# An mLSTM and MLA encoder layer: tokens transposed before their RMS norm, the norm applied to the projections' results, and the opening loads issued at once

## The chip, the cores and the metric

One core of one Trainium2 chip. The metric is the device time of one execution in microseconds, median of three runs. The core has a matrix engine (PE, with its weight loader PEld), a vector engine (DVE), a scalar engine (ACT), a pool engine (POOL) and a sync engine (SP) that here issues nearly all transfers; every engine works through its own instructions in order and waits for others by semaphores.

## The reference

```python
h = rms_norm(x, g_mix)                   # x: 2048 x 1024, float32
z = h @ w_in                             # one projection, split into ten streams
q_m, k_m, v_m, o_m, gates, c_q, c_kv, k_pe = split(z)
qk  = silu(conv_centred([q_m, k_m]))     # depthwise conv of width 5 along the tokens
y_a = mlstm_group(qk, v_m, o_m, gates)   # bidirectional chunkwise mLSTM, 4 heads
y_b = mla_group(c_q, c_kv, k_pe, ...)    # latent attention, 4 heads, full softmax
x = x + concat(y_a, y_b) @ w_out
x = x + square(relu(rms_norm(x, g_ffn) @ w_ff1)) @ w_ff2
def rms_norm(x, g):
    return x * rsqrt(mean(x * x, -1) + 1e-6) * g
```

The norm's factor is one number per token. So `(x * r) @ w` and `(x @ w) * r` are the same but for rounding: the factor can be put on the rows of x or on the rows of the product.

## The kernel before

The program runs in phases; the change lies in `phase_a` alone, which ends at about 464 us of the span. It makes `z = h @ w_in` and its streams. The instructions of `phase_a` are put in order, engine by engine, by a scheduler that simulates the program; the later phases are ordered by hand, and their code is not touched. So the place of an instruction in a queue of `phase_a` is not the place of its line in the code.

Every float32 matrix product is made as three fp32r products (`mm3`, L67 to L69): each operand is split into a high part (`hh`, `wh`), cast by ACT (L52, L55), and a low part (`hl`, `wl`), the rest, which DVE subtracts (L53, L56). A product is hi by hi, hi by lo, lo by hi.

The 2048 tokens are 16 tiles of 128, in two halves of eight. `load_x` loads a tile `xt`; `prep` takes its mean square on ACT (`xjunk`, L145), the inverse root on POOL (`rsqrt`, L62 and L63), multiplies the tile by it on DVE (L148), and transposes it on PE in two groups of four blocks (`pt`, L153), each group being split into `hh` and `hl`, in which 512 tokens lie side by side. For each half, PE then goes through four blocks of columns of `w_in`, each block being eight row tiles k0 to k7 that `load_w` loads (`raw`, L161, three buffers) and splits:

- `rest`: the 464 columns of the gates and of the latents, called CR in the code, one `pz` of 24 matmuls per token tile. DVE adds a bias to the gates (`G`, L259), ACT copies the others (`zr`, L264).
- `z_v` (CV): 512 columns; DVE copies the result (L450) and SP stores it.
- `z_qk` (CQ): here the channels are on the partitions and 512 tokens are the columns. ACT copies the result into `zc` (L407), DVE does the five taps of the conv (L413 to L415).
- `z_o` (CO): ACT takes the sigmoid straight from PSUM (`vo`, L456), DVE multiplies by a gain.

Between them stand the steps of MLA's latents (`mla_a1` to `mla_b2`), by `tick`, and the splits of MLA's up-projections w_uq and w_ukv (`load_wu`: `wuqh`, `wuql`, `wukh`, `wukl`), whose raw tiles use the same three `raw` buffers.

At the very start, SP issues x0, the rows of `g_mix` (turned into columns on PE at L182, since `split` of the weights multiplies by g), three weight tiles, x1, small vectors, and then the further weight tiles as buffers come free.

A form that the change uses is in the kernel already, in the attention: a small SBUF tile with tokens on its partitions is stored to DRAM transposed (`d_rd`, L1036, 128x2, with `rearrange("a p -> p a")`), and read back spread over all partitions (`rb`, L1041).

Of the kernel before, what the change touches and what calls it, by code (L numbers as in the profile page):

```python
# [8 lines left out]
F32 = mybir.dt.float32  # L9
F32R = mybir.dt.float32r  # L10
# [76 lines left out]
def scratch(c, ctx):  # L87
    tc = c.tc
    dr = ctx.enter_context(tc.tile_pool(name="scratch", bufs=1, space=DRAM))
    c.d_qkT = dr.tile([4, P, S], F32, name="d_qkT")  # L90
    c.d_k = dr.tile([S, 256], F32, name="d_k")
    c.d_v = dr.tile([S, 512], F32, name="d_v")
    c.d_sg = dr.tile([S, 512], F32, name="d_sg")
    c.d_qn = dr.tile([NH, P, S], F32, name="d_qn")
    c.d_kn = dr.tile([NH, P, S], F32, name="d_kn")
    c.d_qr = dr.tile([NH, ROPE, S], F32, name="d_qr")
    c.d_kr = dr.tile([NH, ROPE, S], F32, name="d_kr")
    c.d_va = dr.tile([S, 512], F32, name="d_va")
# [17 lines left out]
def phase_a(c):  # L116
    nc, tc = c.nc, c.tc
    with ExitStack() as st:
# [16 lines left out]
        psM = pool("a_psM", 4, space=PSUM)  # L135

        def load_x(t):
            xt = xp.tile([P, D], F32, name="xt")
            nc.sync.dma_start(xt, c.x[t * P:(t + 1) * P, :])
            return xt  # L140

        def prep(t, xt, hh, hl):
            junk = ep.tile([P, D], BF16, name="xjunk", bufs=1)
            ms = sp.tile([P, 1], F32, name="xms")
            nc.scalar.activation(junk, xt, AF.Square, scale=D ** -0.5, accum_out=ms)  # L145
            r = sp.tile([P, 1], F32, name="xr")
            rsqrt(c, r, ms, 1)
            nc.vector.tensor_scalar(xt, xt, r, None, op0=ALU.mult)  # L148
            tt = t % 4
            for g in range(2):  # L150
                pt = psT.tile([P, 4, P], F32, name="pt")
                for k in range(4):
                    nc.tensor.transpose(pt[:, k, :], xt[:, (4 * g + k) * P:(4 * g + k + 1) * P], c.ident)  # L153
                split(nc, hh[:, 4 * g:4 * g + 4, tt * P:(tt + 1) * P],
                      hl[:, 4 * g:4 * g + 4, tt * P:(tt + 1) * P], pt)

        def load_w(c0, n):
            res = []
            for k in range(KD):
                raw = rp.tile([P, 512], F32, name="raw")  # L160
                nc.sync.dma_start(raw[:, :n], c.w_in[k * P:(k + 1) * P, c0:c0 + n])  # L161
                wh = wp.tile([P, 512], F32R, name="wh")
                wl = wp.tile([P, 512], F32R, name="wl")
                split(nc, wh[:, :n], wl[:, :n], raw[:, :n], gmix[:, k:k + 1])
                res.append((wh, wl))
            return res

        def vec_rows(name, srcs, q):

            rows = kp.tile([64, P], F32, name=name)  # L170
            nr = 0
            for src in srcs:
                if len(src.shape) == 2:
                    src = src.rearrange("a b -> (a b)")
                n = src.shape[0] // P
                q.dma_start(rows[nr:nr + n, :], src.rearrange("(r p) -> r p", p=P))
                nr += n
            return rows, nr

        def vec_cols(c0, rows, nr):  # L180
            pt = psT.tile([P, 4, P], F32, name="pt")
            nc.tensor.transpose(pt[:, 0, :nr], rows[:nr, :], c.ident[:nr, :nr])  # L182
            nc.vector.tensor_copy(c.vec[:, c0:c0 + nr], pt[:, 0, :nr])

        xts = {0: load_x(0)}
        gmix, gcq, cb = c.vec[:, 0:8], c.vec[:, 8:11], c.vec[:, 11:15]
        cw = c.vec[:, 15:35].rearrange("p (k c) -> p c k", c=4)
        c.gffn = c.vec[:, 35:43]
        vec_cols(0, *vec_rows("rows0", (c.g_mix,), nc.sync))
        posi = kp.tile([NT, P], I32, name="posi")  # L190
        gq = kp.tile([P, DH], F32, name="gq")
        gk = kp.tile([P, DH], F32, name="gk")
# [63 lines left out]
        def rest(t, hts, w):  # L256
            pz = z_nat(hts, t % 8, w, NR)
            for half, ci in ((0, t), (2, NT - 1 - t)):
                nc.vector.tensor_tensor(  # L259
                    c.G[:, half:half + 2, :, ci],  # L260
                    pz[:, half * 4:half * 4 + 8].rearrange("p (a h) -> p a h", a=2),
                    bg[:, half * 4:half * 4 + 8].rearrange("p (a h) -> p a h", a=2), op=ALU.add)
            zr = zp.tile([P, 448], F32, name="zr")
            nc.scalar.copy(zr, pz[:, 16:NR])  # L264
            return zr

        def rope(dst, src, t, nh, tmp):
# [12 lines left out]

        def mla_a1(t, zr):

            junk = mp.tile([P, 256], BF16, name="mjunk1")
# [18 lines left out]
        def mla_a2(t):  # L302
# [16 lines left out]
            junk = mp.tile([P, 256], BF16, name="mjunk2")  # L319
# [73 lines left out]
        def z_qk(j, ch, hts, w):  # L393
# [10 lines left out]
                nc.vector.memset(zc[:, 0:4], 0.0)  # L404
            else:
                nc.vector.tensor_copy(zc[:, 0:4], carry[:, ch, :])
            nc.scalar.copy(zc[:, 4:516], pz)  # L407
            if last:
                nc.vector.memset(zc[:, 516:518], 0.0)
            else:  # L410
# [16 lines left out]
            if ch >= 2:  # L427
# [12 lines left out]
                if last:  # L440
                    pt = psT.tile([P, 4, P], F32, name="pt")
                    nc.tensor.transpose(pt[0:2, 0, :], ot[:, 512:514], c.ident)
                    k2 = ep.tile([2, P], F32, name="k2", bufs=1)
                    nc.scalar.copy(k2, pt[0:2, 0, :])
                    nc.sync.dma_start(c.d_k[S - 2:S, cs], k2)

        def z_v(t, hts, w):
            pz = z_nat(hts, t % 8, w, 512)
            o = ep.tile([P, 512], F32, name="vo")
            nc.vector.tensor_copy(o, pz)  # L450
            nc.sync.dma_start(c.d_v[t * P:(t + 1) * P, :], o)

        def z_o(t, hts, w):
            pz = z_nat(hts, t % 8, w, 512)
            o = ep.tile([P, 512], F32, name="vo")
            nc.scalar.activation(o, pz, AF.Sigmoid)  # L456
# [6 lines left out]
        def prep_t(t, hts):  # L463
# [3 lines left out]
            if xt is None:  # L467
                xt = load_x(t)
            prep(t, xt, *hts[t % 8 // 4])

        hts = []
        prep_t(0, hts)
        w = load_w(CR, NR)
        xts[1] = load_x(1)
        prep_t(1, hts)
        xts[2] = load_x(2)
        for dst, src in ((bg, c.b_gates), (ivf, c.inv_freq), (gq, c.g_q), (gk, c.g_k), (gmo, c.g_mout)):
            nc.sync.dma_start(dst, bcast(src, P))
        nc.sync.dma_start(posi, c.pos.rearrange("(t p) -> t p", p=P))
# [1 line left out]
        for half in range(2):  # L481
# [1418 lines left out]
```

## Time and profile before

| | |
|---|---|
| median of 3 runs | 2602.04 us (2601.08 to 2602.11) |
| profiled execution | 2599.91 us, of which the span 2598.0 us; granted clock 1.00 |
| PE busy | 2567.6 us, 99% |
| DVE, ACT, POOL busy | 1668.4, 1208.4, 387.5 us |
| PE busy, 0 to 24.97 us | 16.35 us |
| PE busy, 24.97 to 60 us | 32.62 us |
| PE busy, 60 to 385 us | without a gap |
| PE busy, 385 to 466 us | 78.86 of 81.0 us |

In the lines of the profile, L153 is a line of the code, the name before the arrow is the tile written, those behind it are read. In a timeline the first column is the start, the second the length, and a bracket at the end gives how long the engine had been idle and who released it. SPq is SP's queue of transfers: its row is the time of issue, not of the transfer. A matmul's length is longer than its share of PE, since matmuls overlap: two neighbours' starts give the pitch.

### The profile page before, as it was taken

What the parts mean: (1) busy time and instruction counts of PE and PEld (TensorE: products, weight loads), DVE (VectorE), ACT (ScalarE), POOL (GpSimd) and SP (SyncE); (2) the same over time, 40 slices, a digit from 0 to 9 for tenths busy, and PEclk for the clock granted to TensorE, in tenths of its full rate; (3) what the DMA queues carried; (4) which work ended last, traced back from release to release, by engine and by line L of the source; (5) the groups of instructions that cost most, each with busy time, mean ns of one, the idle gap of its engine ahead of it and who ended that gap; (6) DMA issues with size and microseconds to landing.
All of it is one profiled execution on the core that took longest, in us unless ns stands there. A gap on an engine that the chain in (4) does not pass through costs nothing. (4 is left out here: it accounts for less than half of the span.)

```text
span 2598.0 us, 37093 instructions
## 1 busy us (share of the span) xinstructions
PE 2567.6 (99%) x13227; PEld 2166.5 (83%) x13227; DVE 1668.4 (64%) x3206; ACT 1208.4 (47%) x2457; POOL 387.5 (15%) x438
## 2 busy tenths in 40 slices
PE   8999999999999999999999999999999999999999
PEld 7888888788888888888888888878888888888887
DVE  6585566666676757674458777877775477665443
ACT  6454543446656656561135554654554323332332
POOL 2211120123224224120000000000000123222000
PEclk9999999999999999999999999999999999999999
DMA  5344245356446455345674656744446744444552
GB/s 165 116 136 150 94 133 144 63 138 135 95 100 122 86 115 94 87 116 171 208 251 161 197 184 197 257 163 141 157 149 237 253 146 146 146 146 145 209 177 98
DMA packets 298293, 391.57 MB, mean 151 GB/s; under 512 B 33217, under 2 KB 187132, under 8 KB 298108
## 3 DMA queue, kind: packets, MB, share of 16 engines
q1 hardware_dynamic: 295804, 385.01, 50.1%
q10 hardware_dynamic: 2304, 4.20, 0.4%
q8 instruction: 104, 1.70, 0.3%
q14 instruction: 81, 0.66, 0.1%
HBM read 256.94 MB, written 132.17 MB: 150 GB/s over the span
## 5 line engine op out<-in xcount | busy, mean ns | idle before, releaser
L67 PE MATMUL pd<-w2h,uh 128*128 128x512 f32 x896 | 348.7, 389 | 0.1
L68 PE MATMUL pd<-w2l,uh 128*128 128x512 f32 x896 | 348.6, 389 | 0.0
L69 PE MATMUL pd<-w2h,ul 128*128 128x512 f32 x896 | 348.6, 389 | 0.0
L53 DVE TENSOR_TENSOR ul<-ur,uh 128x1024 fp32r<-128x1024 f32 x110 | 154.7, 1406 | 254.9 <-ACT uh L52 254.6
L52 ACT CAST uh<-ur 128x1024 fp32r<-128x1024 f32 x110 | 116.0, 1055 | 395.2 <-PE pd L68 380.9
L53 DVE TENSOR_TENSOR ptl<-ptp,pth 128x512 fp32r<-128x512 f32 x256 | 176.4, 689 | 186.7 <-ACT pth L52 179.1
L52 ACT CAST pth<-ptp 128x512 fp32r<-128x512 f32 x256 | 148.8, 582 | 239.0 <-PE ptp L1050 236.1
L1520 DVE TENSOR_TENSOR e<-pu,e 128x512 f32<-128x512 f32 x224 | 151.2, 688 | 101.3 <-PE pu L69 90.4
L1020 DVE TENSOR_SCALAR_CACHE_REDUCE p<-ps 128x512 f32<-128x512 f32 x256 | 174.9, 684 | 40.4 <-PE ps L1019 37.7
L67 PEld LDWEIGHTS pd<-w2h,uh 128*128 128x128 f32 x896 | 168.2, 188 | 35.4 <-DVE e L1520 0.5
L69 PEld LDWEIGHTS pd<-w2h,ul 128*128 128x128 f32 x896 | 168.2, 188 | 35.0
L68 PEld LDWEIGHTS pd<-w2l,uh 128*128 128x128 f32 x896 | 168.2, 188 | 34.9
L1677 POOL TENSOR_TENSOR r<-wr,r 128x512 f32<-128x512 f32 x48 | 80.0, 1667 | 628.8 <-DMA wr<-in_w 601.9
L1396 ACT CAST r<-w1raw 128x512 fp32r<-128x512 f32 x160 | 98.3, 615 | 125.1 <-PE pu L69 115.4
L1050 PE MATMUL ptp<-ident,p 128*128 128x128 f32 x1024 | 152.8, 272 | 1.3 <-ACT p L1031 0.9
L67 PE MATMUL pz<-wh,hh 128*128 128x512 f32 (+1 forms) x384 | 150.9, 395 | 2.7 <-ACT hh L52 2.7
L68 PE MATMUL pz<-wl,hh 128*128 128x512 f32 (+1 forms) x384 | 149.0, 388 | 1.0 <-DVE wl L56 1.0
L69 PE MATMUL pz<-wh,hl 128*128 128x512 f32 (+1 forms) x384 | 149.5, 390 | 0.0
L68 PE MATMUL pv<-ptl,vh 128*128 128x256 f32 x496 | 140.3, 283 | 2.0 <-DVE ptl L53 1.9
L67 PE MATMUL pv<-pth,vh 128*128 128x256 f32 x496 | 139.9, 282 | 1.5 <-ACT pth L52 1.5
L69 PE MATMUL pv<-pth,vl 128*128 128x256 f32 x496 | 139.9, 282 | 0.0
L1523 ACT ACTIVATE e<-e 128x512 f32<-128x512 f32 x128 | 80.9, 632 | 126.5 <-DVE e L1520 119.8
(403 smaller groups left out, 6569.7 us busy)
## 6 DMA issues: line engine op xcount, KB each, us to landing
d_u<-e SPq DMA_DIRECT2D x224, 256.0 KB
ur<-d_u SPq DMA_DIRECT2D x110, 512.0 KB
w1raw<-in_w SPq DMA_DIRECT2D x64, 512.0 KB
wr<-in_w SPq DMA_DIRECT2D x96, 256.0 KB
raw<-in_w_in SPq DMA_DIRECT2D x48, 256.0 KB
xt<-in_x SPq DMA_DIRECT2D x16, 512.0 KB
mb<-d_M SPq DMA_DIRECT2D x32, 256.0 KB
r<-in_x SPq DMA_DIRECT2D x16, 512.0 KB
```

Source lines behind the costliest of these rows:

```text
L52: nc.scalar.copy(hi, src)
L53: (eng or nc.vector).tensor_tensor(lo, src, hi.bitcast(F32), op=ALU.subtract)
L67: nc.tensor.matmul(out, ah, bh, start=first, stop=False)
L68: nc.tensor.matmul(out, ah, bl, start=False, stop=False)
L69: nc.tensor.matmul(out, al, bh, start=False, stop=last)
L1020: nc.vector.tensor_scalar(probs[b, a][:, j, :], o, SCALE, None, op0=ALU.mult, op1=ALU.max, accum_out=maxes[b, a][:, j:j + 1])
L1050: nc.tensor.transpose(pt[:, k, :], p[:, j, k * P:(k + 1) * P], c.ident)
L1396: self.c.nc.scalar.copy(wh, src)
L1520: nc.vector.tensor_tensor(out, o, t, op=ALU.add)
L1523: nc.scalar.activation(t, t, AF.Relu)
L1677: nc.gpsimd.tensor_tensor(R, wr, R, op=ALU.subtract)
```

## The change

Tiles are transposed raw. A new `norm(t)` takes the mean square, in place, after the transposes, and writes the inverse root into column t of a tile `rinv` (128 x 16). The norm is then applied where the projection's results leave PSUM: by `rinv[:, t]` in `rest`, `z_v` and `z_o`, where a token is a partition; and in `z_qk`, where the tokens are columns, by a tile `rb` that holds the 512 factors on every partition. For that, after each fourth token tile the four columns of `rinv` are stored to DRAM (`d_r`, transposed, 512 elements of 4 bytes), and `load_r` reads them back, spread over the partitions. `load_r` is called twice a half, ahead of the blocks CV, CQ and CO.

The opening's eight raw weight tiles have places of their own (three `raw`, five in the places of later tiles), x2 and x3 are loaded into the places of `wukh` and `wukl`, x0 comes in two pieces from two queues, the rows of g_mix go over ACT's queue, and a dummy Square stands ahead of all ACT work. Three small tiles change their names to share buffers.

```diff
 def load_x(t):
-    xt = xp.tile([P, D], F32, name="xt")
-    nc.sync.dma_start(xt, c.x[t * P:(t + 1) * P, :])
+    xt = kp.tile(..., name=("wukh", "wukl")[t - 2]) if t in (2, 3) else xp.tile([P, D], F32, name="xt")
+    for q, cs in ((nc.sync, slice(0, 512)), (nc.scalar, slice(512, D))) if t == 0 else ((nc.sync, slice(0, D)),):
+        q.dma_start(xt[:, cs], c.x[t * P:(t + 1) * P, cs])
 def prep(t, xt, hh, hl):
-    junk = ep.tile([P, D], BF16, name="xjunk", bufs=1)
-    ms = sp.tile([P, 1], F32, name="xms")
-    nc.scalar.activation(junk, xt, AF.Square, scale=D ** -0.5, accum_out=ms)
-    r = sp.tile([P, 1], F32, name="xr")
-    rsqrt(c, r, ms, 1)
-    nc.vector.tensor_scalar(xt, xt, r, None, op0=ALU.mult)
...
+def norm(t, xt):
+    ms = sp.tile([P, 1], F32, name="xms")
+    nc.scalar.activation(xt, xt, AF.Square, scale=D ** -0.5, accum_out=ms)
+    rsqrt(c, rinv[:, t:t + 1], ms, 1)
+    if t % 4 == 3:
+        nc.sync.dma_start(c.d_r[t - 3:t + 1].rearrange("a p -> p a"), rinv[:, t - 3:t + 1])
+def raw_w(k, c0, n, first=False):
+    if first and k > 2:
+        raw = mp.tile([P, 512], F32, name=("vn", "kn", "kT", "qT", "rT")[k - 3])
+    else:
+        raw = rp.tile([P, 512], F32, name="raw")
+    nc.sync.dma_start(raw[:, :n], c.w_in[k * P:(k + 1) * P, c0:c0 + n])
+    return raw
...
-vec_cols(0, *vec_rows("rows0", (c.g_mix,), nc.sync))
+vec_cols(0, *vec_rows("rows0", (c.g_mix,), nc.scalar))
+nc.scalar.activation(rinv[:, 0:1], c.mhalf[:, 0:1], AF.Square)
 # rest
-        nc.vector.tensor_tensor(c.G[...], pz[...], bg[...], op=ALU.add)
+        nc.vector.scalar_tensor_tensor(c.G[...], pz[...], rinv[:, t:t + 1], bg[...], op0=ALU.mult, op1=ALU.add)
-    nc.scalar.copy(zr, pz[:, 16:NR])
+    nc.scalar.activation(zr, pz[:, 16:NR], AF.Copy, scale=rinv[:, t:t + 1])
 # z_qk
-    nc.scalar.copy(zc[:, 4:516], pz)
+    nc.vector.tensor_tensor(zc[:, 4:516], pz, rbs[j], op=ALU.mult)
 # z_v
-    nc.vector.tensor_copy(o, pz)
+    nc.vector.tensor_scalar(o, pz, rinv[:, t:t + 1], None, op0=ALU.mult)
 # z_o
-    nc.scalar.activation(o, pz, AF.Sigmoid)
+    nc.scalar.activation(o, pz, AF.Sigmoid, scale=rinv[:, t:t + 1])
...
+def load_r(j):
+    rb = rbs[j] = ep.tile([P, 512], F32, name="rb")
+    nc.sync.dma_start(rb, bcast(c.d_r[4 * j:4 * j + 4].rearrange("a p -> (a p)"), P))
 hts = []
+raws = [raw_w(k, CR, NR, True) for k in range(4)]
+xts[1] = load_x(1)
+raws += [raw_w(k, CR, NR, True) for k in range(4, KD)]
+xts[2], xts[3] = load_x(2), load_x(3)
 prep_t(0, hts)
-w = load_w(CR, NR)
-xts[1] = load_x(1)
+w = [split_w(k, raw, NR) for k, raw in enumerate(raws)]
+norm(0, xts.pop(0))
 prep_t(1, hts)
-xts[2] = load_x(2)
...
     nxt = []
+    for j in range(2):
+        load_r(2 * half + j)
     for blk in range(3):
         w = load_w((CV, CQ, CO)[blk], 512)
```

How the change moves instructions shows at three places (rows: line, operation, tile written, tiles read, size; "x8" is eight in a row). The first is SP's queue at the opening: the tiles of x (L139 before, L141 after), the first block's weights (`in_w_in`, 128x464), the rows of g_mix and small vectors (L478, L503). Before:

```order
L139 DMA xt<-in_x 128x1024
L176 DMA rows_134<-in_g_mix 8x128
L161 DMA raw<-in_w_in 128x464 x3
L139 DMA xt<-in_x 128x1024
L478 DMA bg<-in_b_gates 128x16
L478 DMA ivf<-in_inv_freq 128x32
L478 DMA gq<-in_g_q 128x192
L478 DMA gk<-in_g_k 128x192
L478 DMA gmo<-in_g_mout 128x512
L161 DMA raw<-in_w_in 128x464
```

After:

```order
L141 DMA xt<-in_x 128x512
L166 DMA raw<-in_w_in 128x464 x3
L166 DMA vn<-in_w_in 128x464
L141 DMA xt<-in_x 128x1024
L166 DMA kn<-in_w_in 128x464
L166 DMA kT<-in_w_in 128x464
L166 DMA qT<-in_w_in 128x464
L166 DMA rT<-in_w_in 128x464
L141 DMA wukh<-in_x 128x1024
L141 DMA wukl<-in_x 128x1024
L503 DMA bg<-in_b_gates 128x16
```

All eight weight tiles, x1, x2 and x3 now stand ahead of the small vectors, and none of them waits for a buffer; before, five weight tiles and x2 waited for one. PE's order in the opening is nearly the same: x1's eight transposes come as two groups of four, the first three matmuls sooner.

The second is SP's queue behind the opening: the loads of w_uq (L239 before, L251 after), of w_ukv (L244, L256), of the tiles x4 and later (L139, L141), and of the block CV (`raw<-in_w_in` 128x512). Before:

```order
L239 DMA raw<-in_w_uq 128x384 x2
L139 DMA xt<-in_x 128x1024 x2
L239 DMA raw<-in_w_uq 128x384
L244 DMA raw<-in_w_ukv 128x512 x2
L161 DMA raw<-in_w_in 128x512
L139 DMA xt<-in_x 128x1024
L161 DMA raw<-in_w_in 128x512 x2
L139 DMA xt<-in_x 128x1024
L161 DMA raw<-in_w_in 128x512
L139 DMA xt<-in_x 128x1024 x2
L161 DMA raw<-in_w_in 128x512 x8
```

After:

```order
L251 DMA raw<-in_w_uq 128x384
L159 DMA d_r<-rinv 128x4x1
L491 DMA rb<-d_r 128x512
L251 DMA raw<-in_w_uq 128x384
L256 DMA raw<-in_w_ukv 128x512 x2
L166 DMA raw<-in_w_in 128x512 x2
L141 DMA xt<-in_x 128x1024
L166 DMA raw<-in_w_in 128x512 x2
L141 DMA xt<-in_x 128x1024 x3
L159 DMA d_r<-rinv 128x4x1
L491 DMA rb<-d_r 128x512
L166 DMA raw<-in_w_in 128x512 x8
```

Two stores of `d_r`, each with the read of `rb` at once or soon behind it, now stand ahead of the last w_uq tile and ahead of k4 to k7 of CV. In the second half it is so twice more: one pair ahead of the loads of x14 and x15, one ahead of k4 to k7 of that half's CV.

The third is ACT at the same place, from the first splits of w_uq to the casts of x4 (`hh<-pt`). Before:

```order
L264 COPY zr<-pz 128x448
L55 ACTIVATE wuqh_148<-raw,vec 128x384 x2
L55 ACTIVATE wuqh_149<-raw,vec 128x384
L287 ACTIVATE mjunk_1015,ms_1016<-zr 128x256
L287 ACTIVATE mjunk_1015,ms_1016<-zr 128x128
L287 ACTIVATE mjunk_1015,ms_1016<-zr 128x64
L55 ACTIVATE wuqh_149<-raw,vec 128x384
L52 CAST hh<-pt 128x4x128
L55 ACTIVATE wukh<-raw,vec 128x512
L52 CAST hh<-pt 128x4x128
```

After:

```order
L276 ACTIVATE zr<-pz,rinv 128x448
L55 ACTIVATE wuqh_153<-raw,vec 128x384
L55 ACTIVATE wukh<-raw,vec 128x512
L52 CAST hh<-pt 128x4x128
L55 ACTIVATE wukh<-raw,vec 128x512
L52 CAST hh<-pt 128x4x128
L156 ACTIVATE xt,xms<-xt 128x1024
```

Behind the copy of a tile's latents, x4's first cast now stands after two weight splits, the fourth of w_uq and the first of w_ukv, where before it stood after the one of w_uq; and x4's Square (L156) comes behind its casts.

More of the change, by code (lines that the diff above doesn't have):

```diff
@@ L107, in scratch @@
     c.d_h = dr.tile([2, 7, P, 4, 512], F32, name="d_h")
+    c.d_r = dr.tile([NT, P], F32, name="d_r")
     c.d_u = dr.tile([7, FF // 256, P, 2, 512], F32, name="d_u")
@@ L137, in load_x @@
         def load_x(t):
-            xt = xp.tile([P, D], F32, name="xt")
-            nc.sync.dma_start(xt, c.x[t * P:(t + 1) * P, :])
+            xt = kp.tile([P, D], F32, name=("wukh", "wukl")[t - 2]) if t in (2, 3) else xp.tile([P, D], F32, name="xt")
+            for q, cs in ((nc.sync, slice(0, 512)), (nc.scalar, slice(512, D))) if t == 0 else ((nc.sync, slice(0, D)),):
+                q.dma_start(xt[:, cs], c.x[t * P:(t + 1) * P, cs])
             return xt
         def prep(t, xt, hh, hl):
-            junk = ep.tile([P, D], BF16, name="xjunk", bufs=1)
-            ms = sp.tile([P, 1], F32, name="xms")
-            nc.scalar.activation(junk, xt, AF.Square, scale=D ** -0.5, accum_out=ms)
-            r = sp.tile([P, 1], F32, name="xr")
-            rsqrt(c, r, ms, 1)
-            nc.vector.tensor_scalar(xt, xt, r, None, op0=ALU.mult)
             tt = t % 4
@@ L155, in prep, with split_w @@
                       hl[:, 4 * g:4 * g + 4, tt * P:(tt + 1) * P], pt)
-        def load_w(c0, n):
[L158 to L166, printed above, removed]
+        def norm(t, xt):
[11 more added lines that the diff above has]
+            return raw
+        def split_w(k, raw, n):
+            wh = wp.tile([P, 512], F32R, name="wh")
+            wl = wp.tile([P, 512], F32R, name="wl")
+            split(nc, wh[:, :n], wl[:, :n], raw[:, :n], gmix[:, k:k + 1])
+            return wh, wl
+        def load_w(c0, n):
+            return [split_w(k, raw_w(k, c0, n), n) for k in range(KD)]
         def vec_rows(name, srcs, q):
-            rows = kp.tile([64, P], F32, name=name)
+            rows = kp.tile([64, P], F32, name="rows")
             nr = 0
@@ L183, in vec_cols @@
             nc.vector.tensor_copy(c.vec[:, c0:c0 + nr], pt[:, 0, :nr])
+        rinv = gp.tile([P, NT], F32, name="rinv")
         xts = {0: load_x(0)}
@@ L204, in rope_tables @@
             kk = ep.tile([P, 512], F32, name="ot")
-            posr = kp.tile([NT, P], F32, name="posr")
+            posr = kp.tile([64, P], F32, name="rows")[:NT, :]
             nc.vector.tensor_copy(posr, posi)
@@ L258, in rest @@
             for half, ci in ((0, t), (2, NT - 1 - t)):
-                nc.vector.tensor_tensor(
+                nc.vector.scalar_tensor_tensor(
                     c.G[:, half:half + 2, :, ci],
-                    pz[:, half * 4:half * 4 + 8].rearrange("p (a h) -> p a h", a=2),
-                    bg[:, half * 4:half * 4 + 8].rearrange("p (a h) -> p a h", a=2), op=ALU.add)
+                    pz[:, half * 4:half * 4 + 8].rearrange("p (a h) -> p a h", a=2), rinv[:, t:t + 1],
+                    bg[:, half * 4:half * 4 + 8].rearrange("p (a h) -> p a h", a=2), op0=ALU.mult, op1=ALU.add)
             zr = zp.tile([P, 448], F32, name="zr")
-            nc.scalar.copy(zr, pz[:, 16:NR])
+            nc.scalar.activation(zr, pz[:, 16:NR], AF.Copy, scale=rinv[:, t:t + 1])
             return zr
@@ L281, in mla_a1 @@
         def mla_a1(t, zr):
-            junk = mp.tile([P, 256], BF16, name="mjunk1")
+            junk = mp.tile([P, 256], BF16, name="mjunk")
             ms3 = sp.tile([P, 3], F32, name="ms3")
@@ L318, in mla_a2 @@
             ms8 = sp.tile([P, 8], F32, name="ms8")
-            junk = mp.tile([P, 256], BF16, name="mjunk2")
+            junk = mp.tile([P, 256], BF16, name="mjunk")
             qs = [pq[h // 2][:, (h % 2) * DH:(h % 2 + 1) * DH] for h in range(NH)]
@@ L442, in z_qk @@
                     nc.tensor.transpose(pt[0:2, 0, :], ot[:, 512:514], c.ident)
-                    k2 = ep.tile([2, P], F32, name="k2", bufs=1)
+                    k2 = ep.tile([P, 4, P], F32, name="kt", bufs=1)[0:2, 0, :]
                     nc.scalar.copy(k2, pt[0:2, 0, :])
@@ L469, in prep_t @@
             prep(t, xt, *hts[t % 8 // 4])
+            if t:
+                norm(t, xt)
+            else:
+                xts[0] = xt
+        rbs = {}
+        def load_r(j):
+            rb = rbs[j] = ep.tile([P, 512], F32, name="rb")
+            nc.sync.dma_start(rb, bcast(c.d_r[4 * j:4 * j + 4].rearrange("a p -> (a p)"), P))
         hts = []
+        raws = [raw_w(k, CR, NR, True) for k in range(4)]
+        xts[1] = load_x(1)
+        raws += [raw_w(k, CR, NR, True) for k in range(4, KD)]
+        xts[2], xts[3] = load_x(2), load_x(3)
         prep_t(0, hts)
-        w = load_w(CR, NR)
-        xts[1] = load_x(1)
+        w = [split_w(k, raw, NR) for k, raw in enumerate(raws)]
+        norm(0, xts.pop(0))
         prep_t(1, hts)
-        xts[2] = load_x(2)
         for dst, src in ((bg, c.b_gates), (ivf, c.inv_freq), (gq, c.g_q), (gk, c.g_k), (gmo, c.g_mout)):
```

## The prediction

> **What bounds the kernel now.** I read the page's busy times first, then PE's table of waits, then windows over the phase that changes, and last the timeline at each wait.
>
> ```profile
> PE 2567.6 (99%) x13227; PEld 2166.5 (83%) x13227; DVE 1668.4 (64%) x3206; ACT 1208.4 (47%) x2457; POOL 387.5 (15%) x438
> 0.00:24.97 24.97, 16.35 (x82) 13.70 (x83) 12.28 (x25) 14.48 (x25) 4.25 (x16) 1.00 0.68 225
> 24.97:60.00 35.03, 32.62 (x166) 27.58 (x166) 22.89 (x61) 24.19 (x56) 8.11 (x16) 1.00 0.40 127
> PE pt L182 <- DMA rows<-in_g_mix: 4.3, 1, 4.3
> PE pt L153 <- DVE xt L148: 3.0, 1, 3.0
> PE pz L67 <- ACT hh L52: 2.7, 4, 0.9
> PE pt L153 <- DVE hl L53: 1.1, 2, 0.9
> PE pz L68 <- DVE wl L56: 1.0, 1, 1.0
> PE pm L565 <- ACT vo L456: 0.7, 1, 0.7
> ```
>
> PE is busy for all but 30 us, so the 12 us of DVE's multiply (16 by 0.75, below) are not on the path: only idle time of PE, or matmuls at a slow clock, can be won, and a new wait of PE costs in full. In the two windows (length, then busy time of PE, PEld, DVE, ACT, POOL, the granted clock) PE idles 24.97 - 16.35 = 8.6 and 35.03 - 32.62 = 2.4 us, 11.0 together. The first 4.3, until the g_mix rows land, stay about as they are. So at most 6.7 us are to be won up to 60 us, and somewhat more from matmuls that start slowly.
>
> **The opening: -3.8.**
>
> ```profile
> 4.32 1.06 ACT L145 ACTIVATE xjunk<-xt 128x1024 bf16<-128x1024 f32 x1 [2.32 <-DMA xt<-in_x]
> 5.55 0.23 POOL L62 TENSOR_SCALAR xr<-xms 128x1 f32<-128x1 f32 x1 [3.90 <-ACT xjunk L145]
> 5.86 0.57 POOL L63 TENSOR_TENSOR xr<-xr,mhalf 128x1 f32<-128x1 f32 x1
> 6.69 0.75 DVE L148 TENSOR_SCALAR xt<-xt,xr 128x1024 f32<-128x1024 f32 x1
> 7.50 1.97 PE L153 MATMUL pt<-ident,xt 128*128 128x128 f32 x8 [3.00 <-DVE xt L148]
> 10.45 0.59 PE L68 MATMUL pz<-wl,hh 128*128 128x464 f32 x1
> 10.84 0.59 PE L69 MATMUL pz<-wh,hl 128*128 128x464 f32 x1
> 11.66 1.89 ACT L55 ACTIVATE wh<-raw,vec 128x464 fp32r<-128x464 f32 x3 [1.33 <-DMA raw<-in_w_in]
> ```
>
> Square, POOL and multiply hold the first transposes from 4.6, when x0 and the identity are there, to 7.5: 2.9 us go. Then ACT's and DVE's splits pace PE: ACT alone has eight weight casts of 0.63 (1.89 for three) and four casts of 0.56 for x0 and x1, 7.3 us from about 5.4, now without the wait of 1.33 for a third weight tile. Laid out row by row, the eighth weight is split at about 13.5, and the matmuls of z0 to z1 that ended at 24.97 end at about 21.1: -3.8. The ends are 0 (the splits pace it all) and -6.7. The table load at the top stands in front of a wait for x already: nothing.
>
> **The first store: +6.1.** The step that costs is the one the trace of before has only elsewhere: `rinv` goes to DRAM as 4-byte elements, and SP waits for its landing before it issues `rb`. The attention has the same form with 256 elements, the gate tables one with 128 (`d_dec`):
>
> ```profile
> 481.92 0.38 SPq L1036 DMA_DIRECT2D d_rd<-rd  x1
> 490.28 0.33 SPq L1041 DMA_DIRECT2D rb<-d_rd  x1
> 494.55 0.33 SPq L623 DMA_DIRECT2D d_dec<-dec  x1
> 503.22 1.27 SPq L637 DMA_DIRECT2D decb<-d_dec  x2
> SPq L1041 <- DMA d_rd<-rd: 7.9, 1, 7.9
> SPq L1041 <- DMA d_rd<-rd: 118.3, 18, 9.3
> q1 hardware_dynamic: 276, 0.01, 1.3%
> 33.61 0.33 SPq L239 DMA_DIRECT2D raw<-in_w_uq  x1
> 36.05 0.62 ACT L55 ACTIVATE wuqh<-raw,vec 128x384 fp32r<-128x384 f32 x1 [0.89 <-DMA raw<-in_w_uq]
> 36.57 0.56 ACT L52 CAST hh<-pt 128x512 fp32r<-128x512 f32 x1
> ```
>
> The first SPq row of waits is of the window 481 to 491, the second of the whole span. From issue to release: 490.28 - 481.92 = 8.36 us, of which SP waits 7.9 for that DMA alone; the transfers of those 12 us (row of q1) took 1.3% of the DMA engines, so it is not a queue behind others. With 128 elements it is at most 503.22 - 494.55 = 8.67: not in proportion to the count. A weight's load, in whole rows, is used 36.05 - 33.61 = 2.44 us after its issue. Over the whole span SP waits for this form 18 times, 118.3 us in all and up to 9.3, so with loads in flight it can only be longer. For 512 elements I take 8.4 in the steps below, since 128 and 256 cost the same, and add 0.6 for each store on the path at the end; the ends are 2.4 (as the weight's) and 16.7 (twice 8.36).
>
> The Trainium skill, "DMA: Bandwidth & Descriptors", section "Anatomy of one DMA — SWDGE (gpsimd) path", gives a fixed 2.0 us and bytes over 436e3 per us, which for these 2 KB is 2.0 us. The rows of the same form say 8.4, so the page's fit is no guide for them; by it the sum would be that of the first rival. Its "Rules for kernel authors" do say that a non-contiguous last dimension becomes one descriptor per element.
>
> By the same laying out, x3's casts end behind the copy of z1's latents and its Square (1.06 and 0.19) and POOL's 0.8 at about 26.0 (an error of 1 us there moves the sum by as much), so `rb` goes out at 34.4 and the last w_uq tile at 34.7, where before it went at 33.61 although PE was then later by the 3.8. It is cast 2.44 us later, at 37.2 or, behind other work, 37.4; behind it on ACT now stands the first w_ukv cast too (0.72), and only then x4's first cast, at 38.7 to 39.2 against 36.57. DVE has its subtractions in the same order.
>
> ```profile
> 37.19 0.48 PE L67 MATMUL pz<-wh,hh 128*128 128x464 f32 x1 [0.43 <-ACT hh L52]
> 38.81 0.63 PE L153 MATMUL pt<-ident,xt 128*128 128x128 f32 x4 [0.93 <-DVE hl L53]
> 39.20 0.46 PE L69 MATMUL pz<-wh,hl 128*128 128x464 f32 x1
> 39.49 0.37 PE L67 MATMUL pz<-wh,hh 128*128 128x464 f32 x1
> 39.70 0.37 PE L68 MATMUL pz<-wl,hh 128*128 128x464 f32 x1
> 51.38 0.48 PE L67 MATMUL pz<-wh,hh 128*128 128x464 f32 x1 [0.89 <-ACT hh L52]
> 52.23 0.65 PE L153 MATMUL pt<-ident,xt 128*128 128x128 f32 x4 [0.15 <-DVE hl L53]
> ```
>
> So z4's third matmul, at 39.20 before, comes at 41.5: 2.3 behind, which takes the 3.8 won and adds as much, 6.1 in all. PE runs out of z0 to z3 at about 32.6 and idles there some 8 us.
>
> **Up to 60 us: -1.0.** The waits at 51.38 and 52.23, 0.89 and 0.15, were for x's chain through Square, POOL and multiply; tiles now come to PE about 2.6 us after landing sooner, and PE is late. PE stands at +1.3.
>
> **The second store: +4.3.**
>
> ```profile
> 55.87 0.59 ACT L52 CAST hh<-pt 128x512 fp32r<-128x512 f32 x1 [0.81 <-PE pt L153]
> 60.30 4.39 SPq L161 DMA_DIRECT2D raw<-in_w_in  x4
> 62.83 0.72 ACT L55 ACTIVATE wh<-raw,vec 128x512 fp32r<-128x512 f32 x1 [1.07 <-DMA raw<-in_w_in]
> 65.96 0.40 PE L67 MATMUL pz<-wh,hh 128*128 128x512 f32 x1
> ```
>
> x7's second cast ends at 56.46, now 57.8; its Square (1.06 and 0.19) and POOL's 0.8 follow: the store goes at 59.8, `rb` at 68.2, k4 of CV at 68.6 instead of 60.30. Its cast, 2.53 us after issue, ends at 71.7; the first matmul with k4 (65.96 before, 67.3 now) waits 4.4, less 0.1 for overlap. Then k5 to k7 follow at ACT's 0.72 each, PE needing 0.69: no more. PE stands at +5.6.
>
> **The second half: +4.1.** The third store stands ahead of x14's load, which has some 8 to 9 us of reserve: 0.3 (ends 0 and 1). The fourth is as the second. From x15's last transpose, PE has 10 matmuls of 384, 33 of 464 and 14 of 512 columns before it needs k4, 11.7 us; the chain is cast 0.56, Square 1.25, POOL 0.8, store 8.4, issue of `rb` 0.33, load and cast 2.53 and 0.62, and about 1 of other work on ACT: 15.5. The wait is 3.8.
>
> **Behind the projections: +0.9.** The wait L68 of 1.0 for `wl` (at 421.8) should go, as DVE has earlier items there. Among the last accumulators of `z_o`, three more than before follow one in the same PSUM bank; each is a wait like L565's 0.7, one of them half covered: +1.6 (ends 0 and 2.1). And in `z_qk` DVE takes the copy from ACT, 16 by the 686 ns of `vo`'s copy, while `z_v` and `rest` keep their durations. The tightest stretch of it:
>
> ```profile
> 385.00:421.00 36.00, 35.34 (x167) 28.77 (x165) 30.98 (x67) 18.12 (x39) 2.46 (x3) 1.00 0.71 180
> L450 DVE COPY vo<-pz 128x512 f32<-128x512 f32 x16 | 11.0, 686 | 7.5 <-PE pz L69 7.0 <-DMA d_kr<-rT 0.5
> ```
>
> DVE has 30.98 of 36; five channel tiles add 3.4: 34.4 of 36, just enough. I take 0.3 (ends 0 and 3.4). ACT's 16 copies less are worth nothing, at 18.12 of 36.
>
> **The clock: +0.8.** In the opening PE's matmuls have a pitch of 10.84 - 10.45 = 0.39, later 39.70 - 39.49 = 0.21, though the window's granted clock reads 1.00; some nine of them lose about 1.6 us. Only the first pause, of 8 us with a few transposes in it, seems long enough to bring that back, and the casts pace PE behind it: half of 1.6; ends 0 and 4.8 (three pauses).
>
> **The sum.** -3.8 + 6.1 - 1.0 + 4.3 + 0.3 + 3.8 + 0.9 + 1.8 (0.6 for each of the three stores on the path) + 0.8 = +13.2. The profiled execution took 2599.91, 2.1 under the median; the difference is set on the median: 2602.0 + 13.2 = 2615.
>
> **The rivals.**
>
> *The store lands as fast as the weights do,* in 2.4 us. Then no weight is late, and there remain -3.8 - 1.0 + 0.9 = -3.9, so 2598; with the opening's full 6.7 won, 2595. For it speaks only that most transfers of this kernel land so; the rows of the same form speak against it. As three stores lie on the path, each us less on the landing takes 3 off the sum: at about 9.0 - 13.2 / 3 = 4.6 us the change is even, below that it gains. This is also what the Trainium skill's 2.0 us, named above, would make of it. Chance 0.13.
>
> *The landing grows with the number of elements,* to 16.7: 3 times 7.7 more, so 2638. Against it: 128 elements did not land sooner than 256. Chance 0.08.
>
> *The clock drops after each pause.* All three are 3.8 us or longer: 4.0 more, 2619. For it: the opening, after idling from the start, needed until about 11.5 to reach the full pitch. No pause over 3 us within the work is in the trace. The Trainium skill, "TensorE: Matmul & The Clock Gate", section "Part 1: The HAM clock gate", lets the array fall to half its clock after an idle window of about 3.4 us; by that rule the first pause would surely do it and the other two sometimes. Chance 0.18.
>
> *One of the stalls is covered,* because a norm is ready earlier than I laid out or a weight's slack is larger: 4 to 8 less, 2607 to 2611. The second and fourth store's times hang on the chain of one token tile, each good for an error of 2 us. Chance 0.14.
>
> **Chances.** The forecast as it stands, 2611 to 2618, has 0.47. Faster or slower by over 0.2% means 5.2 us, about what a measurement tells from no change: below 2596.8 lies a good third of the first rival, 0.05; between there and 2607.2 the rest of it and a part of the last, 0.12; above, 0.83. The range 2600 to 2628 leaves out most of the first and all of the second rival. The likeliest case alone is 2609 to 2621.
>
> **What would show it.** Right: on SP, `rb` waits some 8 us or more for `d_r` four times, and the w_in loads behind it go out late; among PE's waits `pz` on `wh` or `hh` by ACT has 4 us at the first CV tile of each half and 6 or more ahead of z4; PE's first transposes at 4.6 to 5; z2 starts near 21; no wait for `xt`. PE's busy time up to 24.97 us is then near 20. Wrong: a `d_r` that lands in under 5 us, or CV weights that come early enough although it does not; an opening that saves nothing; `zc` holding up PE in the conv stage.

## The result: 31 us slower, and the profile after

The changed kernel takes 2633.36 us (2632.03 to 2636.05, 4 runs) against 2602.07 for the kernel before (4 runs): a ratio of 1.0121, 95% interval 1.0108 to 1.0133. The forecast was 2615, its range 2600 to 2628: the direction and the place were right, the size was not, 13 us forecast against 31.

First PE's waits after, then windows (length, busy PE, PEld, DVE, ACT, POOL, granted clock, DMA share, GB/s) up to the end of the projections, which PE reaches at 463.86 us before and at 496.49 after; the first row is of before, the others of after.

```profile
PE pz L67 <- ACT wh L55: 17.0, 4, 8.1
PE pz L67 <- ACT hh L52: 9.8, 2, 9.5
```

```profile
0.00:463.80 463.80, 450.70 (x2234) 381.26 (x2234) 285.83 (x738) 221.90 (x655) 71.44 (x127) 1.00 0.43 133
```

```profile
0.00:496.40 496.40, 459.07 (x2234) 388.82 (x2234) 285.92 (x736) 220.04 (x640) 69.54 (x122) 0.97 0.40 126
0.00:24.97 24.97, 20.04 (x96) 17.37 (x97) 11.16 (x25) 16.10 (x33) 4.43 (x16) 1.00 0.72 247
24.97:60.00 35.03, 24.73 (x119) 20.89 (x118) 16.77 (x46) 16.19 (x29) 3.54 (x8) 0.85 0.29 92
60.00:136.00 76.00, 67.92 (x317) 57.63 (x316) 28.95 (x83) 27.89 (x96) 10.33 (x17) 0.93 0.31 96
290.00:385.00 95.00, 86.92 (x424) 74.28 (x423) 43.50 (x128) 39.10 (x133) 14.47 (x24) 0.96 0.29 91
```

The same 2234 matmuls end 32.6 us later, which is all of the loss of the profiled execution but 2 us. PE idles 496.4 - 459.07 = 37.3 instead of 463.8 - 450.7 = 13.1 us: 24.2 more. And it is busy 8.4 us longer for the same work: that is the clock, granted at 0.85, 0.93 and 0.96 in the three windows that hold a long pause. The opening did what was forecast, 20.04 us of work by 24.97 instead of 16.35.

The timeline after, at the first two stores of `d_r`: SP's issues, then ACT's casts of the weights behind them, then PE.

```profile
26.92 0.38 SPq L159 DMA_DIRECT2D d_r<-rinv  x1
35.30 0.33 SPq L491 DMA_DIRECT2D rb<-d_r  x1
35.73 0.37 SPq L251 DMA_DIRECT2D raw<-in_w_uq  x1
...
64.69 0.38 SPq L159 DMA_DIRECT2D d_r<-rinv  x1
74.58 0.33 SPq L491 DMA_DIRECT2D rb<-d_r  x1
75.00 12.51 SPq L166 DMA_DIRECT2D raw<-in_w_in  x8
```

```profile
41.43 0.61 ACT L55 ACTIVATE wuqh<-raw,vec 128x384 fp32r<-128x384 f32 x1 [12.01 <-DMA raw<-in_w_uq]
...
79.96 0.72 ACT L55 ACTIVATE wh<-raw,vec 128x512 fp32r<-128x512 f32 x1 [12.36 <-DMA raw<-in_w_in]
```

```profile
43.38 0.75 PE L67 MATMUL pz<-wh,hh 128*128 128x464 f32 x1 [9.54 <-ACT hh L52]
...
46.55 0.59 PE L67 MATMUL pz<-wh,hh 128*128 128x464 f32 x1
46.94 0.59 PE L68 MATMUL pz<-wl,hh 128*128 128x464 f32 x1
...
80.73 0.79 PE L67 MATMUL pz<-wh,hh 128*128 128x512 f32 x1 [8.08 <-ACT wh L55]
81.33 0.63 PE L67 MATMUL pm<-wukh,cTh 128*128 128x512 f32 x1
81.75 0.63 PE L68 MATMUL pm<-wukl,cTh 128*128 128x512 f32 x1
```

The landing is what the attention's rows had told: 35.30 - 26.92 = 8.4 and 74.58 - 64.69 = 9.9 us. But a weight issued behind it is cast 41.43 - 35.73 = 5.7 and 79.96 - 75.00 = 5.0 us after its issue, not 2.44 and 2.53; and behind each pause PE runs at half pace, a pitch of 0.39 for 464 columns and 0.42 for 512, where 0.21 and 0.23 are usual, until 48.9 and 86.4.

### The profile page after: what moved, and what is told of

It is laid out like the page before. It is cut to its first block, busy times and chain, and to the rows that moved or that the text cites. A ratio compares the mean times of both kernels' runs of the same rounds, so it can differ in the third digit from the quotient of the medians.

```text
span 2632.6 us, 37090 instructions
## 1 busy us (share of the span) xinstructions
PE 2577.4 (98%) x13227; PEld 2175.5 (83%) x13227; DVE 1674.7 (64%) x3206; ACT 1207.7 (46%) x2442; POOL 401.5 (15%) x438
## 5 line engine op out<-in xcount | busy, mean ns | idle before, releaser
L53 DVE TENSOR_TENSOR ul<-ur,uh 128x1024 fp32r<-128x1024 f32 x110 | 141.5, 1286 | 250.3 <-ACT uh L52 250.0
L1704 POOL TENSOR_TENSOR r<-wr,r 128x512 f32<-128x512 f32 x48 | 91.8, 1913 | 618.4 <-DMA wr<-in_w 589.7
L1058 ACT ACTIVATE p<-p,nm 128x2048 f32<-128x2048 f32 x64 | 128.6, 2010 | 22.7 <-DVE nm L1051 22.7
```

The costliest lines, as they stand in the source:

```text
L53: (eng or nc.vector).tensor_tensor(lo, src, hi.bitcast(F32), op=ALU.subtract)
L1058: nc.scalar.activation(p, p, AF.Exp, bias=maxes.pop((b, a)), accum_out=dens[b][:, a:a + 1])
L1704: nc.gpsimd.tensor_tensor(R, wr, R, op=ALU.subtract)
```

## The experiments

Levels drift by some us between sittings (the kernel before stood at 2602.6, 2606.1, 2606.1 and 2603.6 in the four), so each is read by its ratio, and by the time at which PE ends the projections in the profiled execution (463.86 before, 496.49 after).

**The late read.** `rb` takes the buffers of `z_v`'s results and is asked for in the conv block, so nothing waits for `d_r` ahead of the weights.

```diff
-            for j in range(2):
-                load_r(2 * half + j)
...
+                    if blk == 1 and i == 0:
+                        load_r(2 * half)
+                        load_r(2 * half + 1)
...
-            rb = rbs[j] = ep.tile([P, 512], F32, name="rb")
+            rb = rbs[j] = ep.tile([P, 512], F32, name="vo")
```

> The changed kernel, with only the two reads of rb in each half moved: they are issued when the first channel tile of the conv block is near (rb takes the buffers of the results of z_v, so it cannot be issued before), and nothing waits for d_r ahead of the weights. Stores of d_r, norms and opening as in the changed kernel. Theory (SP waits for the landing of d_r, and the weights behind it come late): PE's stalls of 9.5, 8.1 and 7.9 us and the slow matmuls behind them, 33 us in all with the smaller ones, are gone; 2597 to 2600 us. Rival (the time went to the norm's new place itself: DVE, ACT or PE's order): still above 2615 us.

Measured 2624.66, ratio 1.0082 (1.0070 to 1.0095): 9 us of the 31 gone, 22 left; the projections end at 488.33. My theory as it stood, that SP's wait is the cost, fell. The time is the rival's, but not for the rival's cause: the norm stands at its new place in the row store too, which is fast. SP and ACT in this run:

```profile
28.04 0.38 SPq L159 DMA_DIRECT2D d_r<-rinv  x1
29.83 0.33 SPq L251 DMA_DIRECT2D raw<-in_w_uq  x1
```

```profile
40.10 0.61 ACT L55 ACTIVATE wuqh<-raw,vec 128x384 fp32r<-128x384 f32 x1 [9.55 <-DMA raw<-in_w_uq]
```

SP issues the weight 1.8 us behind the store and waits for nothing, and yet it is cast 10.3 us later. The store holds up the transfers behind it.

**The row store.** The same numbers, turned on PE and stored as 4 runs of 512 bytes; `rb` waits at its old place.

```diff
-                nc.sync.dma_start(c.d_r[t - 3:t + 1].rearrange("a p -> p a"), rinv[:, t - 3:t + 1])
+                pt = psT.tile([P, 4, P], F32, name="pt")
+                nc.tensor.transpose(pt[0:4, 0, :], rinv[:, t - 3:t + 1], c.ident)
+                rt = ep.tile([P, 4, P], F32, name="kt", bufs=1)[0:4, 0, :]
+                nc.vector.tensor_copy(rt, pt[0:4, 0, :])
+                nc.sync.dma_start(c.d_r[t - 3:t + 1], rt)
```

> The changed kernel, with only the form of the store changed: the four columns of rinv are turned on PE to 4 rows of 128 and stored as 4 runs of 512 bytes instead of 512 elements of 4 bytes; the read of rb still waits for it at the same place in SP's queue. Theory A (the 4-byte elements make the landing long): it lands in 2 to 3 us, the stalls fall to 0 to 3 us each and the time to 2600 to 2608 us. Theory B (any store that is read back takes 8 us): 2628 to 2636 us.

2597.88, ratio 0.9982 (0.9973 to 0.9991): faster than both kernels, as theory A had it and below its range.

```profile
31.56 0.28 SPq L163 DMA_DIRECT2D d_r<-kt  x1
32.73 0.34 SPq L495 DMA_DIRECT2D rb<-d_r  x1
```

```profile
461.20 0.32 PE L596 MATMUL pm<-ident,G 128*64 128x128 f32 x1 [0.78 <-ACT vo L472]
```

It lands in 1.2 us here (up to 2.6 at the other stores), PE waits once, 0.6 us, for a weight in place of 17.0 us, and the projections end 2.7 us before those of the kernel before. So everything else in the change is worth a small gain, and the whole loss is the store's form.

The store's form also delays what is issued after its landing. GB/s of all transfers in 40 slices of 0.2 us, first in the changed kernel from 35 us, where `rb`'s read went out at 35.30, then with the row store from 32 us, where it went out at 32.73:

```profile
GB/s 0 0 0 0 0 0 0 0 0 0 0 0 0 0 0 0 72 92 195 72 72 61 166 184 274 328 374 371 397 415 399 420 348 266 236 164 10 0 0 0
```

```profile
GB/s 0 10 0 0 0 0 0 0 61 20 205 174 82 182 289 256 202 210 277 361 379 392 208 287 215 236 266 358 317 225 389 369 266 471 328 184 205 215 317 317
```

The first bytes move 2.9 us behind the issue of the read in the changed kernel, and 0.9 us behind it with the row store. The weight behind the read is cast 5.7 us after its issue in the one, 3.7 in the other (33.17 to 36.89).

**The read without a wait.** `rb` is read from the gain `g_mout`, so the read depends on no store; the conv block is multiplied by those numbers instead.

```diff
-            nc.sync.dma_start(rb, bcast(c.d_r[4 * j:4 * j + 4].rearrange("a p -> (a p)"), P))
+            nc.sync.dma_start(rb, bcast(c.g_mout, P))
```

> The changed kernel, with rb read from another tensor of 512 numbers (a gain that is an input), so that the read, of the same size and form, waits for no store; the stores of d_r stay, and nobody waits for them. The conv block is scaled by wrong numbers. Theory (the wait for the landing is the cost): as with the late read, 2597 to 2601 us. Rival (the spread read of 256 KB itself holds up the weights behind it, which in the changed kernel were cast 5 to 5.7 us after their issue instead of 2.5): a stall of 2 to 3 us ahead of z4 stays, and the time is 2602 to 2606 us.

2623.38, ratio 1.0079 (1.0063 to 1.0094); the projections end at 484.04. Neither theory: the first two reads were issued by 19.4 us, and no transfer was left moving when the store was issued at 26.29, yet the w_uq weight, issued at 28.08 behind it, was cast only at 38.62. It agrees with the late read: the store alone makes the weight late.

**The opening alone,** in the kernel before (the `raw_w`, `split_w` and `load_x` of the change, with the norm ahead of the transposes).

> The kernel before, with only the opening's loads of the change (all eight weight tiles, x1, x2 and x3 at once, x0 in two pieces, the rows of g_mix over ACT's queue); the norm stays ahead of the transposes, and there is no d_r. Theory (the opening's gain of 3.4 us comes from both, the norm's chain of 2.9 us taken off the first tile and the weights' earlier landing, 1.3 us of wait): 1 to 2 us faster than before, 2600 to 2601 us. Rival (the loads alone bring it): 3 to 4 us faster, 2598 to 2599 us.

2599.71, ratio 0.9987 (0.9978 to 0.9996). By the trace it gains nothing: PE still waits 4.2 us for the first multiplied tile, and its projections end at 464.67, 0.8 us behind the kernel before. The timed gain of 0.13% is within what later phases differ from execution to execution, and I leave it open.

**The store on ACT's queue,** on top of the late read (`nc.scalar.dma_start` for `nc.sync.dma_start`).

> The kernel with the late read, in which w_uq's tile was cast 10.3 us after its issue although nothing waited for d_r, with the four stores of d_r issued from ACT's queue instead of SP's; still 512 elements of 4 bytes. Theory (a store of 4-byte elements holds up the transfers behind it in its own queue until it has landed): the weights on SP's queue are cast 2.4 to 3 us after their issue again, no stall over 2 us is left ahead of z4 and in the first CV tiles, and the time is 2597 to 2602 us. Rival (it holds up the DMA engines themselves, whatever the queue): the stalls of 6 to 7 us stay, 2620 to 2626 us.

2625.41, ratio 1.0076 (1.0061 to 1.0091), the projections end at 488.62: the rival. ACT's and SP's rows, and the GB/s of all transfers from 26.8 to 36.8 us in 40 slices of 0.25:

```profile
26.39 0.40 ACTq L159 DMA_DIRECT2D d_r<-rinv  x1
...
39.59 0.61 ACT L55 ACTIVATE wuqh<-raw,vec 128x384 fp32r<-128x384 f32 x1 [10.53 <-DMA raw<-in_w_uq]
```

```profile
28.20 0.33 SPq L251 DMA_DIRECT2D raw<-in_w_uq  x1
```

```profile
GB/s 0 0 6 3 0 0 0 0 0 86 6 6 0 0 0 0 0 0 0 0 0 0 49 104 53 100 111 98 57 41 43 43 27 27 57 76 43 55 51 49
```

The 6 and the 3, at 27.3 to 27.8, are the store's own 2 KB. Three weights, 700 KB, wait on another queue than the store's. Still almost nothing but one short burst moves until 32.3, and then 30 to 110 GB/s, and the weight is used 11.4 us after its issue. The hold-up is not one of SP's queue; it reaches the transfers of the other queue as well.

**Runs of 16 bytes.** `d_r` is stored as it lies, one run a partition; the factors come in another order.

```diff
-c.d_r[t - 3:t + 1].rearrange("a p -> p a")
+c.d_r[t - 3:t + 1].rearrange("a p -> (a p)").rearrange("(p a) -> p a", a=4)
```

> The changed kernel, with the store of d_r not transposed: 128 runs of 16 bytes, one a partition, instead of 512 elements of 4 bytes; everything else stays, rb waits at the same place (its numbers come in another order, so the conv block is scaled by wrong factors). Theory A (runs far below 512 bytes are what is slow, whatever their number): landing again 8 to 9 us, 2628 to 2636 us. Theory B (the cost goes with the number of runs): a quarter of 512, but the gate tables' 128 elements also took 8.6 us, so B expects at most 3 us and 2600 to 2608 us.

2608.03, ratio 1.0005 (0.9995 to 1.0014), at the edge of B's range.

```profile
27.84 0.33 SPq L159 DMA_DIRECT2D d_r<-rinv  x1
29.25 0.33 SPq L491 DMA_DIRECT2D rb<-d_r  x1
29.68 0.37 SPq L251 DMA_DIRECT2D raw<-in_w_uq  x1
```

```profile
34.74 0.61 ACT L55 ACTIVATE wuqh<-raw,vec 128x384 fp32r<-128x384 f32 x1 [4.39 <-DMA raw<-in_w_uq]
```

128 runs of 16 bytes land in 1.4 us here (1.4 to 3.3 over the four). That takes most of the loss away, but not all: by ratio this form stands 0.2%, some 6 us, behind the row store, and in its profiled execution, the slowest of its ten, the projections end at 472.96, 9.1 us behind the kernel before. The weight behind the spread read of 256 KB is cast 5.1 us after its issue, where it is 2.4 in the run without transfers below and 3.7 with the row store and the same read. So the read can account for 1.3 us at most; what comes on top, here and in the changed kernel, goes with the store's form.

**The row store in 512 runs of 4 bytes, and in 16 of 128.** From the same 4 partitions, interleaved in DRAM (l = 1 or 32); the factors come in another order.

```diff
+c.d_r[t - 3:t + 1].rearrange("a p -> (a p)").rearrange("(n a l) -> a n l", a=4, l=1)
```

> The kernel with the row store, from the same 4 partitions and with the same 512 numbers, but interleaved in DRAM, so that it is 512 runs of 4 bytes again (the factors come in another order, so the conv block is scaled wrongly). Theory A (short runs are slow): rb goes out 8 us or more after the store's issue. Theory C (the 128 source partitions, 32 transfers a DMA engine, are slow, and not the runs' length): 1 to 3 us as with the row store.

> As the interleaved row store, with 16 runs of 128 bytes. Theory A, if every run below 512 bytes is slow: 8 us from issue to the issue of rb. If only the number of runs counts (16 against 512): 1 to 3 us, as the row store's 1.2 to 2.4 us.

One execution each: 2644.52 and 2600.27, with the kernel before at 2606.1; the projections end at 498.07 and 461.82. SP with 4 bytes, then with 128:

```profile
32.11 0.28 SPq L163 DMA_DIRECT2D d_r<-kt  x1
40.95 0.33 SPq L495 DMA_DIRECT2D rb<-d_r  x1
```

```profile
31.70 0.28 SPq L163 DMA_DIRECT2D d_r<-kt  x1
32.92 0.33 SPq L495 DMA_DIRECT2D rb<-d_r  x1
```

8.8 against 1.2 us (up to 11.2 and 2.5 at the other stores). The weight behind the read is cast 5.9 us after its issue with 4 bytes and 3.9 with 128. It is not the number of source partitions, and not every run below 512 bytes.

**Four stores added to the kernel before,** first straight from x's tile, then from a small tile of their own in three forms: 512 elements of 4 bytes, 128 runs of 16 bytes, 128 elements of 4 bytes. Nobody reads them.

```diff
+            if tt == 3:
+                x4 = gp.tile([P, 4], F32, name=f"x4{t}")
+                nc.vector.tensor_copy(x4, xt[:, 0:4])
+                nc.sync.dma_start(c.d_r[t - 3:t + 1].rearrange("a p -> p a"), x4)
```

> The kernel before, with only four stores added to SP's queue, one behind each fourth tile's multiply: 512 elements of 4 bytes (four columns of x's tile), to a DRAM tensor that nobody reads. No read, no norm moved. Theory (while 4-byte elements are being written, the transfers of every queue come late by 8 us or more): the last w_uq tile is cast 8 to 11 us after its issue instead of 2.4, and k4 of CV likewise; the stalls ahead of z4 and in the first CV tile of each half are 4 to 7 us and the time 2612 to 2624 us. Rival (the hold-up needs the reads or the new order of the changed kernel): 2600 to 2605 us.

> The kernel before, with four stores added that nobody reads, each of 512 elements of 4 bytes, from a small tile of its own (DVE copies four columns of x's tile to it), so that no buffer is held until the store lands, as x's was in the run before this. Theory (while such a store is under way the transfers of all queues come late): x5, issued behind the first store, lands 11 us or more after its issue instead of 3.6, PE waits some us for x's tiles and for weights, 2610 to 2622 us. Rival (only the wait for the landing, of SP or of a buffer, costs): 2601 to 2604 us.

> The same with each store as 128 runs of 16 bytes. If the element of 4 bytes is what holds up the others: x5 lands 3.6 to 4.5 us after its issue, 2601 to 2604 us. If any small run does: as with 512 runs of 4 bytes.

> The same with each store as 128 elements of 4 bytes (one column). If the hold-up is a matter of the 4-byte element and not of their number, as the landing of 8.4 us for 256 and 8.7 for 128 suggests: as with 512 elements, 2610 to 2622 us. If it goes with the number: a quarter of the loss, 2603 to 2607 us.

The first took 2633.85, ratio 1.0105 (1.0091 to 1.0119), above both ranges, but for a mixed reason: x5's load waited for x's buffer until the store of it had landed (22.86 to 31.75). With tiles of their own the ratios are 1.0086 (1.0071 to 1.0101), 1.0014 (1.0004 to 1.0024) and 1.0067 (1.0052 to 1.0083). For each of the three, the store's issue and x5's behind it, then the Square that waits for x5:

```profile
23.85 0.38 SPq L154 DMA_DIRECT2D d_r<-x  x1
25.73 0.34 SPq L140 DMA_DIRECT2D xt<-in_x  x1
...
38.04 1.06 ACT L146 ACTIVATE xjunk<-xt 128x1024 bf16<-128x1024 f32 x1 [8.56 <-DMA xt<-in_x]
```

```profile
23.28 0.33 SPq L154 DMA_DIRECT2D d_r<-x  x1
25.48 0.33 SPq L140 DMA_DIRECT2D xt<-in_x  x1
...
30.45 1.06 ACT L146 ACTIVATE xjunk<-xt 128x1024 bf16<-128x1024 f32 x1 [1.20 <-DMA xt<-in_x]
```

```profile
23.65 0.33 SPq L154 DMA_DIRECT2D d_r<-x  x1
25.05 0.33 SPq L140 DMA_DIRECT2D xt<-in_x  x1
...
36.17 1.06 ACT L146 ACTIVATE xjunk<-xt 128x1024 bf16<-128x1024 f32 x1 [7.12 <-DMA xt<-in_x]
```

From issue to use: 12.3, 5.0 and 11.1 us (at most 3.8 before, where ACT did not wait for it). So four unread stores of 2 KB cost 22 us in the kernel before; a quarter of the elements still costs 17, and the same 128 runs at 16 bytes 4; the projections end at 485.64, 480.45 and 467.91. The element of 4 bytes counts far more than the number. What no run tells is whether it is the size of the element or its neighbourhood: each of these stores fills whole rows of 512 bytes, so that elements next to each other in DRAM are written one by one, and elements lying far apart were not tried. Two of the three missed their ranges by a few us: the 16-byte form costs 1.2 us of x5's landing and a lower clock behind it (0.95 granted from 24.97 to 60 us), and 512 elements some us more than I allowed.

**The row store with the late read, with the old opening, and no transfer at all** (DVE multiplies by a resident gain).

> The changed kernel with the row store (4 runs of 512 bytes) and the late read of rb, so that neither a slow store nor the spread read of 256 KB stands ahead of the weights. If the spread read costs PE nothing more (row store with the read at its old place has no wait of PE on a weight left), it equals the row store alone, 2596 to 2599 us; if it still cost, 1 to 2 us less than that.

> The changed kernel with the row store, but with the opening of the kernel before (weights loaded as buffers come free, x2 and x3 by the two buffers of x). So it has the norm behind the transposes alone. The row store with the new opening took 2597.9, the new opening alone 2599.7 (its trace stood 0.8 behind the kernel before at the end of the projections, though). Theory (the two parts need each other: the norm's chain goes and then the weights' landing binds): 2599 to 2602 us. Rival (the norm's move does all of it): 2597 to 2598 us.

> The changed kernel without d_r and rb: no store and no read; DVE multiplies the conv block by a tile that is in SBUF anyway (a gain, so the factors are wrong). It is what the change would give if the factors' way cost nothing. Theory: 2595 to 2598 us, as the row store less at most 2 us. Rival (DVE's 16 multiplies or the norm's new place cost more than a microsecond or two): above 2600 us.

2602.59, 2606.35 and 2599.00, all above the ranges named, but with the kernel before at 2606.1, where the ranges were set with it at 2602.6. Ratios 0.9991 (0.9982 to 1.0000), 1.0001 (0.9992 to 1.0009) and 0.9976 (0.9966 to 0.9986); scaled by them to 2602.6 the third falls into its range and the first two stay about 1 us above. By the trace the projections end at 460.95, 462.51 and 460.49, against 463.86 before and 461.20 with the row store. By these single traces the read's place is worth 0.3 us, and the way of the factors by rows costs some 0.7. The norm behind the transposes gains 1.4 us with the old opening, the opening alone loses 0.8, both together gain 2.7: it seems that each takes away the wait behind which the other's gain was hidden. Behind the projections, whose code is the same, these executions differ by up to 11 us (2134.1 us in the kernel before, 2145.3 with the old opening); why is open, and so their whole times decide nothing here.

## Why the prediction was right in kind and wrong in size

- **The opening, -3.8:** right. z2 starts at 21.5 instead of 24.8: -3.3.
- **The landing of `d_r`, 8.4 and 0.6:** nearly right: 8.4, 9.9, 8.4 and 10.5, of which the first, second and fourth lie on the path, 28.8 us where the sum had 27.0. The rows of the same form carried the forecast. The Trainium skill's 2.0 us ("DMA: Bandwidth & Descriptors", "Anatomy of one DMA — SWDGE (gpsimd) path") is fitted to the path by way of gpsimd, and these stores went by SP; here 4-byte elements took four to five times as long, and the row store landed in 1.2 to 2.6 us.
- **The rivals:** the fast landing did not come; nor did the landing that grows with the number. The even point, a landing of some 4.6 us, was not met by any run, and it rests on SP's wait alone: with runs of 16 bytes, which land in 1.4 to 3.3 us, the gain that it promises did not come (ratio 1.0005).
- **Failed: the load behind the store, "2.44 us after its issue".** I priced the store as a wait of SP and gave the weights behind it the row of an undisturbed load. They took 5.7 and 5.0 us. The spread read ahead of them, which I had given no price, can be 1.3 of the first (3.7 with the row store and the same read); the other 2.0 go with the store's form, by which nothing moves until 2.9 us behind the issue of that read. So z4's third matmul came at 46.02 instead of 41.5: the store went out 0.9 later than laid out, at 26.92, the weight issued at 35.73 was cast 3.3 later than 2.44 us would have had it, and the rest is the slow pitch. The two CV waits were 8.1 and 7.9 instead of 4.3 and 3.8. The deeper miss is the mechanism: with SP's wait taken away (late read) 9 us of the loss go and 22 stay, by the hold-up of the other transfers. In the changed kernel the two lie on top of each other, so the wait alone seemed to explain it, and a store that nobody waits for would have been costed at nothing.
- **Failed: the clock, +0.8.** All three pauses brought back the slow pitch, as the third rival had it, and at some 2.8 us each, 8.4 in all, not the 1.6 each of that rival: the slow stretches lasted 4.2 to 5.7 us, where nine matmuls at a pitch of 0.39 are 3.5. The Trainium skill's half clock after an idle window of about 3.4 us ("TensorE: Matmul & The Clock Gate", "Part 1: The HAM clock gate") agrees with each of the three pauses of 7.9 to 9.5 us and pitches of 0.39 against 0.21; the second and third were twice as long as I had laid out.
- **The second half:** besides the 7.9 there are small waits (1.5 for x's tile, 1.4 and 1.1 for `vo`'s banks, 1.0 for weights); the banks were in the sum, at 1.6.
- **`z_qk` on DVE:** near enough, at 0.3: the changed kernel has one wait of 1.1 on a copy in the conv block, and with the row store PE has none.

At the end of the projections the sum missed by 32.6 - 13.2 = 19.4 us. The clock is 8.4 - 0.8 = 7.6 of it. The other 11.8 are idle time of PE, 24.2 where the sum had 12.4: 3.2 and 3.5 at the two CV waits (8.1 and 7.9 against 4.9 and 4.4, each with its 0.6), some 3 ahead of z4, and the small waits.

## What to carry to other kernels

Before a few numbers are sent through DRAM transposed, element by element, look for any such store in the profile you have: its landing is seen at whoever waits for it, and its hold-up at everybody else's transfers, also on other queues. Turn the tile on PE and store rows; runs of 16 bytes avoid most of the loss, but some us of it stayed here. When a stall is costed, price the transfers behind it by a row measured in the same company, and add the clock that a pause of several us takes away.

## What the runs showed of the hardware that I had not expected

- A store of 4-byte elements to packed rows of DRAM landed 8.4 to 11.2 us after its issue with 512 elements (13.0 once, in the first run of added stores), 8.4 with 256 (SP's waits for that form reach 9.3) and at most 8.7 with 128, whether from 4 partitions or from 128; runs of 16, 128 and 512 bytes landed in 1.2 to 3.3.
- While it is under way other transfers nearly stop, on its queue and on another: loads issued 1.4 to 1.9 us behind it are used 10 to 12 us after issue, and total traffic stays near 0, but for a short burst, for 4 to 6 us and then mostly below 125 GB/s for several more. In the changed kernel nothing moved for 2.9 us even behind the landing of the first store. Its own packets took 2.5% of the engines' time in the 10 us from 26.8 (store on ACT's queue), so its share of the DMA engines does not show it. What inside the transfers' path waits, no run here can tell.
- A weight behind a store of `d_r` and the read of 2 KB spread over 128 partitions (256 KB) is used 3.7 us after issue with rows, 5.1 with 16 bytes and 5.7 with 4 bytes, against 2.4 without either. No run separates the read from the store.
